# The last pair of a QKV projection: copy order, whole-block stores, and a remainder copied by two engines

## The chip, the cores and the metric

The kernel runs on one core of a Trainium2 chip. The metric is device time in microseconds of one execution. Engines: TensorE (PE in the profile; its weight loads are PEld), VectorE (DVE), ScalarE (ACT), GpSimd (POOL) and SyncE (SP), which computes nothing and issues most of the DMAs. ScalarE issues a few DMAs too; they stand in its own instruction order (ACTq in the profile, SPq for SP's).

## The reference

```python
batch, seq, hidden = 16, 512, 768
x     = np.random.randn(batch, seq, hidden).astype(np.float32)
w_qkv = np.random.randn(hidden, 3 * hidden).astype(np.float32)

qkv = np.matmul(x, w_qkv)
q, k, v = qkv[..., :768], qkv[..., 768:1536], qkv[..., 1536:]
return np.stack([q, k, v], axis=0)
```

An 8192 x 768 matrix times a 768 x 2304 matrix. The result is cut by columns into three outputs of 768 columns that lie one behind the other in memory.

## The kernel before

**Tiling.** The 8192 rows are taken in 32 pairs of 128-row tiles (`NP = 32`; a pair is 256 rows). The 2304 columns are taken as two wide groups of 1024 columns, columns 0 to 1023 and 1280 to 2303 (`Q_OFF = (0, 1280)`, two blocks of 512 each, `CB = 512`), and a remainder of 256 columns between them (`REM`). A pair and a wide group make a `quad`: a 2 x 2 block matrix with the blocks c11, c12, c21 and c22, each 128 rows x 512 columns, kept in one SBUF tile `u.o` until it is stored.

**Seven products.** A quad is computed by a Strassen-like scheme with seven half-depth products instead of eight. Products 1 and 2 use bf16 copies; products 3 to 7 use sums of weight blocks (`ts`) and sums of x blocks (`sr`). A product is three matmuls of 128x128 by 128x512 (`product`, L258). Products accumulate in PSUM banks: 1, 6, 7 and 4 in the bank `u.x`, 5 and 3 in `u.y`, 2 in `u.z`. `do(u, n)` runs one product and then copies or adds the bank to the block that it completes:

- product 1 is copied to c11 by ScalarE (L267), product 2 added to it by VectorE (L280);
- after product 6 the bank `u.x` is copied to c12 by ScalarE (L286); after product 3 VectorE adds `u.y` to c12 (L299);
- after product 7 ScalarE copies `u.x` to c22 (L292), and VectorE adds `u.y` (which holds product 5) to it (L293);
- after product 4 ScalarE copies `u.x` to c21 (L296).

**Order.** The instructions of each engine stand in the order in which the code issues them. Waits between engines are semaphores, put in from what each instruction reads and writes. Every DMA also takes one of eight completion semaphores in turn, and a DMA whose semaphore is still that of an earlier transfer waits, on the engine that issues it, until that one has landed.

**The end.** `plain` and `summed` handle the pairs in the middle. The two quads of the pair before the last are stored block by block with `store_cols` (from `plain` with `stored`, and from `summed` with `"parts"`). The last pair is `last(a, b)`: a is its columns 0 to 1023, b its columns 1280 to 2303. TensorE's order there is: product 1 of a and b, the remainder of the first row tile, product 2 of a and b, 6 of a and b, 5 and 7 of a, 5 and 7 of b, then 4 and 3 of a, 4 and 3 of b, and the remainder of the second row tile. Stores follow each finished block. `store_cols` cuts a block where it crosses from one of the three outputs into the next: c12 and c22 of a (columns 512 to 1023, a border at 768) and c11 and c21 of b (columns 1280 to 1791, a border at 1536) are two DMAs of 128x256 each. All go from SP, but c21 of a and the first half of c21 of b, which go from ScalarE. `rem_stored` computes the remainder of one row tile in six matmuls (L316), copies 128x256 with ScalarE (L414) and stores it from ScalarE (L416). L690 is the end of the program, where SP waits for all DMAs and the engines meet at a barrier.

Of the kernel before, what the change touches and what calls it, by code (L numbers as in the profile page):

```python
# [10 lines left out]
def kernel(  # L11
# [20 lines left out]
    nc = tc.nc  # L32
    P = 128
    G = 32
    B, T, H = x.shape
    M = B * T
# [5 lines left out]
    NP = M // (2 * P)  # L42
    CB = 512
    REM = N3 - 4 * CB
    Q_OFF = (0, 2 * CB + REM)
# [4 lines left out]
    ident = mybir.ActivationFunctionType.Identity  # L50
    add = mybir.AluOpType.add
# [3 lines left out]
    out_flat = out.rearrange("s b t h -> s (b t) h")  # L55
# [184 lines left out]
    def quad(p, q, pool=o_pool, tag="o"):  # L240
        u = Quad()
        u.p, u.q = p, q
        u.o = pool.tile([P, 2, 2 * CB], fp32, name="o", tag=tag)
        u.x = u.y = u.z = None
        return u

    def product(u, n, ps, start):
        t1, t2, t3, t4 = ts[u.q]
        if n <= 2:
            h = (n - 1) * KH  # L250
            lhs = [xb[u.p][:, h + j, :P] for j in range(KH)]
            rhs = [b1[u.q][:, h + j, :] for j in range(KH)]
        else:
            k, t = {3: (4, b22[u.q][:]), 4: (0, t4), 5: (1, t1), 6: (2, t2), 7: (3, t3)}[n]
            lhs = [sr[u.p][:, k, j, :] for j in range(KH)]
            rhs = [t[:, j, :] for j in range(KH)]
        for j in range(KH):
            nc.tensor.matmul(  # L258
                ps[:], lhs[j], rhs[j],
                start=(start and j == 0), stop=(j == KH - 1), skip_group_check=True,  # L260
            )

    def bank():
        return ps_pool.tile([P, CB], fp32, name="ps")

    def evacuate(u):
        nc.scalar.activation(u.o[:, 0, :CB], u.x[:], ident)  # L267

    def do(u, n, out=True):
        c11, c12 = u.o[:, 0, :CB], u.o[:, 0, CB:]  # L270
        c21, c22 = u.o[:, 1, :CB], u.o[:, 1, CB:]
        if n == 1:
            u.x = bank()
            product(u, 1, u.x, True)
            if out:
                evacuate(u)
        elif n == 2:
            u.z = bank()
            product(u, 2, u.z, True)
            nc.vector.tensor_tensor(c11, c11, u.z[:], op=add)  # L280
        elif n == 6:
            first = u.x is None
            if first:
                u.x = bank()
            product(u, 6, u.x, first)
            nc.scalar.activation(c12, u.x[:], ident)  # L286
        elif n == 5:
            u.y = bank()
            product(u, 5, u.y, True)
        elif n == 7:  # L290
            product(u, 7, u.x, False)
            nc.scalar.activation(c22, u.x[:], ident)  # L292
            nc.vector.tensor_tensor(c22, c22, u.y[:], op=add)  # L293
        elif n == 4:
            product(u, 4, u.x, False)
            nc.scalar.activation(c21, u.x[:], ident)  # L296
        elif n == 3:
            product(u, 3, u.y, False)
            nc.vector.tensor_tensor(c12, c12, u.y[:], op=add)  # L299
# [14 lines left out]
    def rem_row(p, r, ps):  # L314
        for j in range(KT):
            nc.tensor.matmul(  # L316
                ps, xb[p][:, j, r * P:(r + 1) * P], w_rem[j // KH][:, j % KH, :],
                start=(j == 0), stop=(j == KT - 1), skip_group_check=True,
            )
# [15 lines left out]
    def two(a, b, early, u=None):  # L335

        do(a, 1)
        do(b, 1, u is None)
        if u is None:
            early()  # L340
            rem(a.p)()()
        else:
            middle(u)
            copied = rem(a.p, between=lambda: third(u))
            evacuate(b)
            early()
            copied()()
            fourth(u)
            load_x(a.p + 3, nc.sync)
        do(a, 2)  # L350
        do(b, 2)
        summed(a, b)

    def summed(a, b, between={}, store=True):

        parts = {7: (1, CB, 2 * CB), 4: (1, 0, CB), 3: (0, CB, 2 * CB)}
        for i, (u, n) in enumerate(
            ((a, 6), (b, 6), (a, 5), (a, 7), (b, 5), (b, 7), (a, 4), (a, 3), (b, 4), (b, 3))
        ):
            do(u, n)  # L360
            if store == "parts" and n in parts:
                store_cols(u, *parts[n], nc.sync)
            elif n == 3 and store:
                store_quad(u)
            between.get(i, lambda: None)()
# [14 lines left out]
    def plain(a, b, c, d, early, rem_c, stored=False):  # L380

        add_first(a)
        add_first(b)
        rem(a.p)()()
        do(c, 1)
        do(d, 1)
        early()
        rem_c()
        do(c, 2)
        do(d, 2)  # L390
        add_second(a)
        add_second(b)
        if stored:
            for u in (c, d):
                store_cols(u, 0, 0, CB, nc.sync)

    def store_cols(u, r, lo, hi, *engs):

        c = Q_OFF[u.q] + lo
        end = Q_OFF[u.q] + hi  # L400
        while c < end:
            n = min(end, (c // H + 1) * H)
            row = (2 * u.p + r) * P
            engs[0].dma_start(
                out_flat[c // H, row:row + P, c % H:c % H + n - c],
                u.o[:, r, c - Q_OFF[u.q]:n - Q_OFF[u.q]],
            )
            c, engs = n, engs[1:] + engs[:1]

    def rem_stored(p, r):  # L410
        ps = bank()
        rem_row(p, r, ps[:, :REM])
        o = or_pool.tile([P, 2, REM], fp32, name="orem")
        nc.scalar.activation(o[:, 0, :], ps[:, :REM], ident)  # L414
        row = (2 * p + r) * P
        nc.scalar.dma_start(out_flat[1, row:row + P, R_OFF - H:R_OFF - H + REM], o[:, 0, :])  # L416

    def last(a, b):

        do(a, 1)  # L420
        do(b, 1)
        rem_stored(a.p, 0)
        for u in (a, b):
            do(u, 2)
            store_cols(u, 0, 0, CB, nc.sync)
        do(a, 6)
        do(b, 6)
        for u in (a, b):
            do(u, 5)
            do(u, 7)  # L430
            store_cols(u, 1, CB, 2 * CB, nc.sync)
        for u in (a, b):
            do(u, 4)
            store_cols(u, 1, 0, CB, *((nc.scalar, ) if u is a else (nc.scalar, nc.sync)))
            do(u, 3)
            store_cols(u, 0, CB, 2 * CB, nc.sync)
        rem_stored(a.p, 1)
# [132 lines left out]
    u = quad(2, 0)  # L570
# [72 lines left out]
    for p in range(ND + 3, NP - 1, 2):  # L643
        first = p == ND + 3
# [13 lines left out]
        a, b = quad(p, 0), quad(p, 1)  # L658
        summed(a, b, {5: turned} if first else {}, False)
        c, d = quad(p + 1, 0), quad(p + 1, 1)  # L660
        final = p + 3 >= NP
        plain(a, b, c, d, early, lambda: rem(c.p)()(), final)
        summed(c, d, {} if final else {0: lambda: transpose(p + 3, 2, 0)}, "parts" if final else True)
    last(quad(NP - 1, 0), quad(NP - 1, 1))


# [28 lines left out]
```

## Time and profile before

| what | value |
|---|---|
| time, median of 3 runs | 359.57 us (359.56 to 359.70) |
| the profiled execution's own time | 359.33 us |
| its span (first to last instruction on the core) | 357.5 us |
| TensorE busy | 352.0 us (98%) |
| VectorE busy | 263.9 us (74%) |
| ScalarE busy | 185.0 us (52%) |
| GpSimd busy | 177.3 us (50%) |
| DMA | 108.10 MB, mean 302 GB/s |
| granted TensorE clock | 1.0 |
| last product's matmuls and last remainder's end (ScalarE starts on it) | 353.73 us |
| stores of single blocks (L404) | 22 from SP, 2 from ScalarE |

How to read it: the times inside the profile count from the start of the span. 1.8 us of the profiled execution's time lie outside the span. A DMA-issuing instruction (DMA_DIRECT2D) shows how long the issuing engine was held, not how long the data took; the time from issue to landing is given by other views. In the views by stretch, the DMA share is the mean busy share of the 16 DMA engines and can come out a little over 1.

### The profile page before, as it was taken

To read this page: it belongs to the slowest core of one execution; us is meant where nothing else is said; L and a number is where in the kernel's file an instruction comes from. 1 tells how busy PE (TensorE), PEld (TensorE's weight loads), DVE (VectorE), ACT (ScalarE), POOL (GpSimd) and SP (SyncE) were. 2 spreads that over 40 slices of the span, in tenths; PEclk is the share of its full clock that TensorE was granted. 3 is DMA by queue.
4 is the path that set the end of the run, shared out by engine and by line. 5 is a ranking of instruction groups with operands and counts; after the bars stand their busy time and mean duration, and the time that the engine had idled before them with its cause. 6 is when DMAs were issued, how large, how long until landed. Compare 5 with 4: busy or idle time off the path is not lost.

```text
span 357.5 us, 5339 instructions
## 1 busy us (share of the span) xinstructions
PE 352.0 (98%) x1776; PEld 252.1 (71%) x1776; DVE 263.9 (74%) x308; ACT 185.0 (52%) x317; POOL 177.3 (50%) x184
## 2 busy tenths in 40 slices
PE   8999999999999999999999999999999999999995
PEld 3474677768677686877768677686877768677674
DVE  3789876796877869777695877869777695877643
ACT  4587755445454653645445454653645455454653
POOL 0031773376466453666535466453666535466420
PEclk9999999999999999999999999999999999999999
DMA  7997999999989998999979899798999979896497
GB/s 296 376 357 236 334 373 340 368 325 342 313 297 340 278 346 206 338 271 307 348 198 386 220 335 312 223 389 215 351 247 329 322 208 386 221 319 247 175 355 265
DMA packets 82203, 108.10 MB, mean 302 GB/s; under 512 B 5120, under 2 KB 62208, under 8 KB 82176
## 3 DMA queue, kind: packets, MB, share of 16 engines
q1 hardware_dynamic: 75072, 102.39, 85.6%
q10 hardware_dynamic: 7104, 5.38, 5.6%
q8 instruction: 14, 0.23, 0.3%
q14 instruction: 13, 0.11, 0.1%
HBM read 32.24 MB, written 75.50 MB: 301 GB/s over the span
## 4 chain that ended last, share of the span: by engine, by line
PE 97%; DMA 2%; ACT 0%; SPq 0%; issue 0%
PE ps L258 79%; PE ps L316 12%; PE ps L486 6%; DMA xin<-in_x_dram 2%; PE ps L185 0%; ACT xc L166 0%; SPq L162 0%; ACT orem L414 0%
## 5 line engine op out<-in xcount | busy, mean ns | idle before, releaser
L258 PE MATMUL ps<-t,s 128*128 128x512 f32 x720 | 177.9, 395 | 0.0
L258 PEld LDWEIGHTS ps<-t,s 128*128 128x128 f32 x720 | 135.0, 188 | 29.6 <-ACT o L267 0.2
L155 DVE STREAM_TRANSPOSE xf<-xin 128x768 f32<-128x768 f32 (+1 forms) x45 | 93.3, 2075 | 2.9 <-DMA xin<-in_x_dram 2.9
L258 PE MATMUL ps<-b,xb 128*128 128x512 bf16 x360 | 85.4, 380 | 0.0
L293 DVE TENSOR_TENSOR o<-o,ps 128x512 f32<-128x512 f32 x58 | 39.9, 687 | 55.2 <-ACT o L292 55.2
L205 POOL CAST xb<-xf 128x1536 bf16<-128x1536 f32 x28 | 41.1, 1466 | 57.0 <-DVE xf L155 57.0
L225 POOL TENSOR_TENSOR s<-xf 128x384 fp32r<-128x384 f32 x29 | 31.0, 1067 | 72.7 <-DVE xf L155 71.0
L258 PEld LDWEIGHTS <-xb 128*128 128x128 bf16 x360 | 33.9, 98 | 36.8 <-issue 4.2
L292 ACT ACTIVATE o<-ps 128x512 f32<-128x512 f32 x58 | 34.7, 598 | 43.6 <-PE ps L258 43.6
L299 DVE TENSOR_TENSOR o<-o,ps 128x512 f32<-128x512 f32 x60 | 41.1, 687 | 20.0 <-PE ps L258 18.8
L258 PE MATMUL ps<-b,s 128*128 128x512 f32 x180 | 50.6, 389 | 0.0
L296 ACT ACTIVATE o<-ps 128x512 f32<-128x512 f32 x60 | 35.9, 598 | 24.6 <-PE ps L258 22.1
L373 DVE TENSOR_TENSOR o<-o,ps 128x512 f32<-128x512 f32 x78 | 47.8, 681 | 0.0
L316 PE MATMUL ps<-w_rem,xb 128*128 128x256 bf16 x384 | 47.3, 273 | 0.0
L286 ACT ACTIVATE o<-ps 128x512 f32<-128x512 f32 x60 | 35.9, 599 | 19.2 <-PE ps L258 15.5
L316 PEld LDWEIGHTS <-xb 128*128 128x128 bf16 x384 | 37.4, 98 | 11.4 <-issue 0.5
L330 ACT ACTIVATE orem<-ps 128x512 f32<-128x512 f32 x31 | 18.5, 597 | 49.5 <-PE ps L316 35.2
L258 PEld LDWEIGHTS ps<-b,s 128*128 128x128 f32 x180 | 33.8, 188 | 7.1
L226 POOL TENSOR_TENSOR s<-s,xf 128x384 fp32r<-128x384 f32 x29 | 29.5, 1019 | 2.3
L227 POOL TENSOR_TENSOR s<-xf 128x384 fp32r<-128x384 f32 x29 | 29.5, 1016 | 0.0
L229 POOL TENSOR_TENSOR s<-xf,s 128x384 fp32r<-128x384 f32 x29 | 29.3, 1009 | 0.0
L377 ACT ACTIVATE o<-ps 128x512 f32<-128x512 f32 x26 | 15.5, 598 | 16.8 <-PE ps L258 16.1
(46 smaller groups left out, 158.6 us busy)
## 6 DMA issues: line engine op xcount, KB each, us to landing
out_dram<-o SPq DMA_DIRECT2D x60, 768.0 KB, 4.6
out_dram<-o SPq DMA_DIRECT2D x67, 256.0 KB, 3.7
xin<-in_x_dram SPq DMA_DIRECT2D x88, 192.0 KB, 5.7
out_dram<-orem SPq DMA_DIRECT2D x31, 256.0 KB, 2.3
xin<-in_x_dram ACTq DMA_DIRECT2D x24, 192.0 KB, 4.5
st<-in_w_qkv_dram SPq DMA_DIRECT2D x5, 768.0 KB, 8.0
out_dram<-o SPq DMA_DIRECT2D x15, 128.0 KB, 2.7
xin<-in_x_dram SPq DMA_DIRECT2D x2, 768.0 KB, 4.9
```

The source lines that it names most:

```text
L155: nc.vector.transpose(turned[:, g:g + n], rows[:, g:g + n])
L205: nc.gpsimd.tensor_copy(out=xb[p][:], in_=xf[p][:])
L225: 1: lambda g: g.tensor_tensor(s[:, 1], a21, a22, op=add),
L226: 2: lambda g: g.tensor_tensor(s[:, 2], s[:, 1], a11, op=sub),
L258: nc.tensor.matmul(ps[:], lhs[j], rhs[j], start=(start and j == 0), stop=(j == KH - 1), skip_group_check=True,)
L286: nc.scalar.activation(c12, u.x[:], ident)
L292: nc.scalar.activation(c22, u.x[:], ident)
L293: nc.vector.tensor_tensor(c22, c22, u.y[:], op=add)
L296: nc.scalar.activation(c21, u.x[:], ident)
L299: nc.vector.tensor_tensor(c12, c12, u.y[:], op=add)
L316: nc.tensor.matmul(ps, xb[p][:, j, r * P:(r + 1) * P], w_rem[j // KH][:, j % KH, :], start=(j == 0), stop=(j == KT - 1), skip_group_check= ...
L373: dve.tensor_tensor(c, c, u.z[:], op=add)
```

## The change

It has three parts, all in the last stretch of the program.

First, for the last pair only, c22 is put together in the other order. Product 5 is complete before product 7, so ScalarE copies `u.y` to c22 after product 5, and VectorE adds `u.x` after product 7.

Second, `store_cols` takes one engine and stores every block in one DMA. A block that crosses the border of two outputs is described as 128 rows x 2 pieces x 256 columns, where the step between the pieces leads from the end of a row in one output to the start of the same row in the next. It is also used for the pair before the last. In `last`, c21 of a is stored from ScalarE as before, and c21 of b whole from SP.

Third, `rem_stored`, which is used for the two row tiles of the last pair, copies the remainder's left 128 columns with ScalarE and its right 128 columns with VectorE; both read one PSUM bank. The store stays on ScalarE.

```diff
         elif n == 5:
             u.y = bank()
             product(u, 5, u.y, True)
+            if u.p == NP - 1:
+                nc.scalar.activation(c22, u.y[:], ident)
         elif n == 7:
             product(u, 7, u.x, False)
-            nc.scalar.activation(c22, u.x[:], ident)
-            nc.vector.tensor_tensor(c22, c22, u.y[:], op=add)
+            if u.p == NP - 1:
+                nc.vector.tensor_tensor(c22, c22, u.x[:], op=add)
+            else:
+                nc.scalar.activation(c22, u.x[:], ident)
+                nc.vector.tensor_tensor(c22, c22, u.y[:], op=add)
...
-    def store_cols(u, r, lo, hi, *engs):
+    def store_cols(u, r, lo, hi, eng):
 
         c = Q_OFF[u.q] + lo
-        end = Q_OFF[u.q] + hi
-        while c < end:
-            n = min(end, (c // H + 1) * H)
-            row = (2 * u.p + r) * P
-            engs[0].dma_start(
-                out_flat[c // H, row:row + P, c % H:c % H + n - c],
-                u.o[:, r, c - Q_OFF[u.q]:n - Q_OFF[u.q]],
-            )
-            c, engs = n, engs[1:] + engs[:1]
+        n = hi - lo
+        row = (2 * u.p + r) * P
+        src = u.o[:, r, lo:hi]
+        left = (c // H + 1) * H - c
+        if left >= n:
+            dst = out_flat[c // H, row:row + P, c % H:c % H + n]
+        else:
+            assert 2 * left == n
+            first = out_flat[c // H, row:row + P, c % H:H]
+            dst = bass.AP(first.tensor, first.offset, [[H, P], [M * H - H + left, 2], [1, left]])
+            src = src.rearrange("m (s n) -> m s n", s=2)
+        eng.dma_start(dst, src)
 
     def rem_stored(p, r):
         ps = bank()
         rem_row(p, r, ps[:, :REM])
         o = or_pool.tile([P, 2, REM], fp32, name="orem")
-        nc.scalar.activation(o[:, 0, :], ps[:, :REM], ident)
+        half = REM // 2
+        nc.scalar.activation(o[:, 0, :half], ps[:, :half], ident)
+        nc.vector.tensor_copy(out=o[:, 0, half:], in_=ps[:, half:REM])
...
-            store_cols(u, 1, 0, CB, *((nc.scalar, ) if u is a else (nc.scalar, nc.sync)))
+            store_cols(u, 1, 0, CB, nc.scalar if u is a else nc.sync)
```

## The prediction

> **What bounds the kernel now.** I read the chain of waits first, then the last 20 us in the timeline, then the same stretch cut into half microseconds, then the waits and landings of the stores. The chain, from the page:
>
> ```profile
> PE 97%; DMA 2%; ACT 0%; SPq 0%; issue 0%
> ```
>
> TensorE sets the time until its last matmul. The edits leave its instructions and their order alone, so only what follows it, and what prepares that, can move. The tail in the timeline:
>
> ```profile
> 348.98 0.60 ACT L292 ACTIVATE o<-ps 128x512 f32<-128x512 f32 x1 [0.76 <-PE ps L258]
> 349.61 0.69 DVE L293 TENSOR_TENSOR o<-o,ps 128x512 f32<-128x512 f32 x1 [2.62 <-ACT o L292]
> 350.34 0.60 ACT L292 ACTIVATE o<-ps 128x512 f32<-128x512 f32 x1 [0.76 <-PE ps L258]
> ...
> 350.97 0.69 DVE L293 TENSOR_TENSOR o<-o,ps 128x512 f32<-128x512 f32 x1 [0.67 <-ACT o L292]
> ...
> 353.06 0.69 DVE L299 TENSOR_TENSOR o<-o,ps 128x512 f32<-128x512 f32 x1 [0.67 <-PE ps L258]
> ...
> 353.73 0.38 ACT L414 ACTIVATE orem<-ps 128x256 f32<-128x256 f32 x1 [0.75 <-PE ps L316]
> 354.15 0.34 ACTq L416 DMA_DIRECT2D out_dram<-orem  x1
> ```
>
> See: each c22 is ready 0.60 + 0.03 + 0.69 us after its last product; c12 of b at 353.75; the remainder's store goes at 354.15. The half microseconds (from, to, length, busy times, clock, DMA share, GB/s):
>
> ```profile
> 350.50:351.00 0.50, 0.50 (x4) 0.42 (x3) 0.03 (x1) 0.44 (x1) 0.00 (x0) 1.00 0.06 23
> 351.00:351.50 0.50, 0.50 (x3) 0.39 (x3) 0.50 (x1) 0.48 (x1) 0.00 (x0) 1.00 0.64 229
> 351.50:352.00 0.50, 0.50 (x4) 0.41 (x3) 0.46 (x2) 0.12 (x1) 0.00 (x0) 1.00 0.76 264
> 352.00:352.50 0.50, 0.50 (x4) 0.42 (x3) 0.39 (x1) 0.12 (x1) 0.00 (x0) 1.00 0.11 33
> 352.50:353.00 0.50, 0.50 (x5) 0.23 (x4) 0.00 (x0) 0.48 (x1) 0.00 (x0) 1.00 0.94 369
> ...
> 356.00:356.50 0.50, 0.00 (x0) 0.00 (x0) 0.00 (x0) 0.00 (x0) 0.00 (x0) 1.00 0.44 164
> ```
>
> See: the DMA engines are nearly idle at 350.5 and at 352.0, then full from 352.5 without a gap until about 356.2 (the last row's 164 GB/s are 82 KB, 0.21 us at the 385 GB/s of the rows before it). So the end is a backlog of stores that began at 352.5: 1.4 MB, not one late instruction. From SP's waits and the landing view of the store issued at 354.52:
>
> ```profile
> SPq L404 <- DMA out_dram<-o: 0.7, 1, 0.7
> DMA to landing us min/median/max: 2.2/2.2/2.2
> ```
>
> The last store (c12 of b) was ready at 353.75, stood 0.7 us behind a reused completion semaphore, and landed at 356.7; the other 0.8 us to the span's end (357.5) is the closing barrier. What a merged store costs, by its nearest rows: the same shape (128x2x256, 256 KB), alone at 331.59:
>
> ```profile
> L331 SPq DMA_DIRECT2D out_dram<-orem x1: 373/373/373, 331.6 to 331.6; - x1
> DMA to landing us min/median/max: 2.1/2.1/2.1
> ```
>
> what the engines moved then (half-microsecond view, other bounds):
>
> ```profile
> 332.40:333.30 0.90, 0.90 (x11) 0.81 (x9) 0.90 (x2) 0.51 (x1) 0.00 (x0) 1.00 0.82 291
> ```
>
> and the four in a row on SP:
>
> ```profile
> 336.14 0.37 SPq L306 DMA_DIRECT2D out_dram<-o  x1
> 336.56 0.46 SPq L307 DMA_DIRECT2D out_dram<-o  x1
> 337.13 0.96 SPq L310 DMA_DIRECT2D out_dram<-o  x1
> 338.14 0.89 SPq L311 DMA_DIRECT2D out_dram<-o  x1
> ```
>
> See: alone it takes 0.37 us to issue, moves its bytes from 0.85 to 1.7 us after issue (0.9 us at 291 GB/s, not 385), and lands at 2.1; the third and fourth in a row hold SP for 0.9 each.
>
> **The change, part by part.** a and b are the two column halves of the last pair; times are of the profiled execution (span 357.5, 359.33 with what lies around it; the runs' median, 359.57, is 0.24 higher, and I carry differences over to it).
>
> *c22.* ScalarE copies the bank of product 5 while product 7 runs: 348.30 to 348.90 for a (products are 0.68 apart), and ScalarE is idle then. VectorE adds product 7's bank at 348.98 instead of 349.61, so c22 of a is ready at 349.67 (was 350.30), of b at 351.03 (was 351.66): 0.63 earlier each. The cover is 0.05 us thin (348.93 against 348.98), but if it is gone c22 is late by just that. New order to mind: product 4 now overwrites a bank that VectorE, not ScalarE, has read. Its earliest start is 350.34 for a, the read ends at 349.67; TensorE loses nothing. Nor does product 3, whose bank is read by 348.90.
>
> *One transfer for each block.* Four blocks of each pair straddle two outputs: the 24 stores of the last two pairs (22 from SP, 2 from ScalarE's queue) become 16, all but one from SP. The pair before the last is issued by 349 with or without this; its cost is nil while SP is free by 349.67 (now it is free from 349.3, and has less to do). In the last pair c22 of a is one issue (0.37) instead of two; c22 of b stays one and goes at 351.06 (was 351.69); c21 of a is unchanged on ScalarE's queue at 351.65; c12 of a goes at 352.42, as now, but whole; c21 of b, now halved between ScalarE's queue (353.01) and SP (353.36), goes whole from SP at 353.01. Behind it on SP waits c12 of b, ready at 353.75. With fewer stores the completion semaphore that it reuses belongs to a store that landed some 4 us before, so the 0.7 us wait goes; what is late next is SP's own issue or the backlog. c21's issue ends at 353.47 if it takes 0.46 as second in a row, at 354.0 if 0.96 as third: c12 of b goes at 353.78 or 354.0.
>
> *The remainder.* Two engines copy halves, but not side by side: as built, VectorE's half waits on the count that ScalarE's half raises, and the store waits on VectorE. ScalarE 128x128: 0.38 for 256 columns, 0.60 for 512, so 0.28. VectorE 128x128 from PSUM is in no row: 0.17 (a quarter of the 0.69 of 128x512) to 0.35 (a 128x384 copy from PSUM); I take 0.25, between casts of 384 and 512 columns drawn down to 128 (0.22) and the upper end. 353.73 + 0.28 + 0.03 + 0.25 + 0.03 = 354.32: the store goes 0.17 later than now (0.09 to 0.27). ScalarE has nothing behind it. The first remainder does the same at 345.0 with VectorE idle until 345.66: nil. The Trainium skill (PSUM — Partial Sum Buffer, PSUM bank collisions raise a hardware error) says that two engines may not read the same partitions of one bank at once, which speaks against the gain from two copiers; in parallel the copy would be 0.1 shorter than now. No run shows such a collision.
>
> *The sum.* Backlog by arrival, first bytes 0.85 after issue: c22 of a 350.5 to 351.4; c22 of b 351.9 to 352.5; c21 of a to 353.2; c12 of a can start at 353.3. So the 512 KB that now open the backlog at 352.5 are nearly out of the way, and about 0.5 us is won up to here. Then two merged stores follow each other from SP. If each moves its bytes in 0.87 to 0.9 as the lone one did, they end at 355.0 to 355.1; c12 of b and the remainder (393 KB at 385 GB/s: 1.02) drain by 356.03 to 356.12 against 356.21 now. Gain 0.09 to 0.18; I take 0.15: 359.57 - 0.15 = 359.42.
>
> **The rivals.** *The merged stores flow at full rate (−0.5).* For: the DMA engines, when full, carried 385 GB/s of 1 KB pieces too. Against: the lone store's 291. Then c12 of a drains at 353.98, c21 of b 354.66, c12 of b 355.34, the remainder 355.68: 0.53 less, 359.04. Its floor is the remainder: issued at 354.32, landing in 1.7 us at the soonest (what a 128 KB store at 350.33 took), 356.0 against 356.7, so at most 0.7 gained, 358.9. [...]
>
> *SP becomes the bound (slower).* c21 of b now stands wholly in front of c12 of b on SP. It decides from the point where the issues of c12 of a and c21 of b end after 354.52, when the last store goes now: 2.1 us for both. At the 0.9 of the third and fourth above they end by 354.4, just short. The same shape at L310 held SP for up to 1.86 us when the engines had a backlog: c21 of b would end at 354.9 to 355.3, c12 of b land 0.4 to 0.8 later than now: 360.0 to 360.4. Against: that is a third store in a row, c21 here a second.
>
> *The gap does not matter (no change).* If pieces of 1 KB set the pace everywhere, at 1.0 us per merged store, the drain ends at 356.3: 359.65.
>
> **How the numbers follow.** Paced merged stores, −0.2 to +0.1: 0.60 (the no-change rival is its upper edge). Full rate, −0.45 to −0.7: 0.25. SP-bound, +0.1 to +0.8: 0.15. Prediction 359.4; the range, 358.95 to 359.75, leaves out the bottom edge of the second and most of the third. About 0.2% (0.72 us) is what a measurement of this kernel can tell from no change: to gain that the remainder's floor must be beaten, 0.04; to lose that takes nearly the longest stall on record, 0.04; within it 0.92.
>
> **What would show it.** VectorE's add of c22 within 0.05 us of product 7's end, no ScalarE step between; SP issuing c22 of b near 351.06 and c12 of b near 353.8 with no semaphore wait; VectorE's half of the remainder starting after ScalarE's ends, store at 354.2 to 354.4; no DMA gap at 352.0, but a rate under 385 GB/s from 353.3 to 355. Full rate there means the first rival; a c21 issue over 1 us on SP the second. TensorE's last matmul off 353.7 by more than 0.1 would mean that something ahead of the tail moved, which I exclude.

## The result and the profile after

The changed kernel takes 358.94 us in the median, the kernel before 359.55 us beside it; the ratio is 0.9984, 95% interval 0.9978 to 0.9990. (One of the 22 executions of the kernel before took 737.67 us; the ratio leaves it out.) That is 0.61 us less, 0.16% by the ratio: in the predicted direction, within the 0.2% that was called no clear change, but four times the 0.15 us that was forecast. Carried over to 359.57, as the prediction does it, the saving gives 358.96, at the very edge of the stated range (358.95 to 359.75). The profiled execution's span fell from 357.5 to 357.0 us.

The tail of the changed kernel in the timeline (start, length, engine, line, operation; in brackets the idle time before it and what ended it):

```profile
348.28 0.60 ACT L291 ACTIVATE o<-ps 128x512 f32<-128x512 f32 x1
349.04 0.69 DVE L295 TENSOR_TENSOR o<-o,ps 128x512 f32<-128x512 f32 x1 [2.12 <-PE ps L258]
...
350.39 0.69 DVE L295 TENSOR_TENSOR o<-o,ps 128x512 f32<-128x512 f32 x1 [0.67 <-PE ps L258]
...
353.05 0.69 DVE L304 TENSOR_TENSOR o<-o,ps 128x512 f32<-128x512 f32 x1 [0.67 <-PE ps L258]
353.71 0.28 ACT L423 ACTIVATE orem<-ps 128x128 f32<-128x128 f32 x1 [0.75 <-PE ps L321]
354.02 0.29 DVE L424 COPY orem<-ps 128x128 f32<-128x128 f32 x1 [0.29 <-ACT orem L423]
354.35 0.34 ACTq L426 DMA_DIRECT2D out_dram<-orem  x1
```

ScalarE starts on the last remainder at 353.71, before the change at 353.73: TensorE did not move. VectorE's add to c22 begins at 349.04 and 350.39 instead of 349.61 and 350.97, right after product 7. The remainder's two copies stand one behind the other, and its store goes at 354.35, 0.2 us later than before.

The DMA traffic of the changed kernel by half microseconds (the last two columns are the share of the 16 DMA engines and GB/s):

```profile
351.50:352.00 0.50, 0.50 (x4) 0.42 (x3) 0.32 (x1) 0.10 (x1) 0.00 (x0) 1.00 0.10 37
352.00:352.50 0.50, 0.50 (x4) 0.42 (x3) 0.37 (x1) 0.14 (x1) 0.00 (x0) 1.00 1.01 393
352.50:353.00 0.50, 0.50 (x5) 0.23 (x4) 0.00 (x0) 0.46 (x1) 0.00 (x0) 1.00 1.06 406
353.00:353.50 0.50, 0.50 (x7) 0.36 (x4) 0.46 (x1) 0.00 (x0) 0.00 (x0) 1.00 0.91 338
353.50:354.00 0.50, 0.18 (x2) 0.00 (x0) 0.23 (x1) 0.28 (x1) 0.00 (x0) 1.00 1.07 377
354.00:354.50 0.50, 0.00 (x0) 0.00 (x0) 0.29 (x1) 0.00 (x0) 0.00 (x0) 1.00 1.10 387
354.50:355.00 0.50, 0.00 (x0) 0.00 (x0) 0.00 (x0) 0.00 (x0) 0.00 (x0) 1.00 1.10 406
...
355.50:356.00 0.50, 0.00 (x0) 0.00 (x0) 0.00 (x0) 0.00 (x0) 0.00 (x0) 1.00 0.48 164
```

The engines are full from 352.0, half a microsecond earlier than before, and empty at about 355.7 (164 GB/s in the last row are 0.21 us at full rate), also half a microsecond earlier. Between 353.3 and 355.0 the two merged stores of c12 of a and c21 of b and the start of c12 of b pass, from 353.5 on at 377 to 406 GB/s. The prediction had set 291 to 300 for them.

SP's waits in the same stretch hold no wait for a DMA in front of a store any more (L416 is the store; L700 is the end of the program):

```profile
SPq L700 <- DMA out_dram<-o: 1.6, 3, 0.6
SPq L416 <- DVE o L304: 1.2, 2, 0.9
```

### The profile page after: what moved, and what is told of

The parts are those of the page before. It is cut to its first block, busy times and chain, and to the rows that moved or that the text cites. A ratio compares the mean times of both kernels' runs of the same rounds, so it can differ in the third digit from the quotient of the medians.

```text
span 357.0 us, 5315 instructions
## 1 busy us (share of the span) xinstructions
PE 350.6 (98%) x1757; PEld 252.1 (71%) x1776; DVE 264.4 (74%) x310; ACT 185.0 (52%) x317; POOL 177.3 (50%) x184
## 4 chain that ended last, share of the span: by engine, by line
PE 74%; POOL 15%; DVE 6%; issue 3%; DMA 2%; ACT 0%; SPq 0%
PE ps L258 56%; PE ps L321 12%; PE ps L496 6%; DVE xf L155 6%; POOL xb L205 5%; POOL s L226 3%; POOL s L225 3%; POOL s L227 3%; DMA xin<-in_x_dram 2%; PE ps L185 0%; DVE o L304 0%; ACT xc L166 0%; SPq L162 0%; DVE orem L424 0%; ACT orem L423 0%
## 5 line engine op out<-in xcount | busy, mean ns | idle before, releaser
L258 PE MATMUL ps<-b,xb 128*128 128x512 bf16 x343 | 81.6, 379 | 1.1
L298 DVE TENSOR_TENSOR o<-o,ps 128x512 f32<-128x512 f32 x56 | 38.5, 688 | 50.7 <-ACT o L297 50.0
L304 DVE TENSOR_TENSOR o<-o,ps 128x512 f32<-128x512 f32 x60 | 41.1, 687 | 20.5 <-PE ps L258 19.4
L378 DVE TENSOR_TENSOR o<-o,ps 128x512 f32<-128x512 f32 x78 | 47.8, 680 | 0.0
```

Source lines behind the costliest of these rows:

```text
L258: nc.tensor.matmul(ps[:], lhs[j], rhs[j], start=(start and j == 0), stop=(j == KH - 1), skip_group_check=True,)
L378: dve.tensor_tensor(c, c, u.z[:], op=add)
```

## The experiments

Several kernels have their last matmul a few tenths of a microsecond earlier or later in the profiled execution, whatever their tail. So beside the time I compare the **tail**: from ScalarE's start on the last remainder to the end of the span. Each tail is that of one execution; three kernels whose times do not differ (before, whole-block stores alone, two copiers alone) agree within 0.04 us. All edits lie in the last pair's code or in the stores of the last two pairs. "Time" is the median against that of the kernel before in the same series.

| kernel | tail, us | time, us | ratio, 95% interval |
|---|---|---|---|
| before | 357.51 − 353.73 = 3.78 | | |
| changed | 357.02 − 353.71 = 3.31 | 358.94 (359.55) | 0.9984 (0.9978 to 0.9990) |
| c22 order alone | 357.47 − 354.02 = 3.45 | 359.12 (359.45) | 0.9993 (0.9984 to 1.0002) |
| whole-block stores alone | 357.63 − 353.81 = 3.82 | 359.45 (359.45) | 1.0001 (0.9992 to 1.0010) |
| two copiers alone | 357.96 − 354.14 = 3.82 | 359.52 (359.45) | 0.9999 (0.9991 to 1.0008) |
| changed, one copier | 357.52 − 354.21 = 3.31 | 358.92 (359.45) | 0.9985 (0.9976 to 0.9994) |
| changed, c22 of b stored late | 358.08 − 354.08 = 4.00 | 359.81 (359.69) | 1.0004 (0.9995 to 1.0013) |
| changed, blocks cut, all on SP | 358.12 − 354.29 = 3.83 | 359.73 (359.69) | 1.0003 (0.9994 to 1.0012) |
| changed, blocks cut, two queues | 357.94 − 354.49 = 3.45 | 359.48 (359.76) | 0.9992 (0.9983 to 1.0001) |
| products a, then b | 358.69 − 355.47 = 3.22 | 360.20 (359.69) | 1.0012 (1.0004 to 1.0021) |
| products by kind | 357.56 − 354.18 = 3.38 | 359.45 (359.75) | 0.9994 (0.9985 to 1.0003) |

The first theory, F: the end is a backlog of store traffic, and what counts is when its first bytes move. Its rivals: S, the gain comes from the completion semaphore on which the last store no longer waits; M, it comes from having one transfer per block.

### The c22 order alone

```diff
+            if u.p == NP - 1:                  # after product 5
+                nc.scalar.activation(c22, u.y[:], ident)
...
+            if u.p == NP - 1:                  # after product 7
+                nc.vector.tensor_tensor(c22, c22, u.x[:], op=add)
```

(added to the kernel before; the stores and the remainder as they were)

> Only the copy order of c22 is changed; blocks are cut into two stores as before, the remainder is copied by ScalarE alone. Theory F (the end is a backlog of bytes, and what counts is when its first bytes move): c22 of b is stored at about 351.1, the DMA engines are full from 351.9 and drained by about 355.7; 0.5 to 0.6 us under the kernel before, the whole gain of the full change. Theory S (the gain comes from the 0.7 us that c12 of b no longer waits for a reused completion semaphore): here the last store still reuses the semaphore of c21 of a, so less than 0.3 us. Theory M (one transfer per block is what pays): 0 to 0.2 us.

The tail is 3.45, 0.33 us of the whole 0.47, and the time 0.33 us less, with an interval that just touches 1. The traffic of this kernel (here ScalarE starts on the remainder at 354.02):

```profile
352.00:352.50 0.50, 0.50 (x4) 0.40 (x3) 0.50 (x1) 0.00 (x0) 0.00 (x0) 1.00 0.48 188
352.50:353.00 0.50, 0.50 (x4) 0.35 (x2) 0.18 (x1) 0.33 (x1) 0.00 (x0) 1.00 1.06 410
...
353.50:354.00 0.50, 0.48 (x5) 0.19 (x2) 0.50 (x1) 0.00 (x0) 0.00 (x0) 1.00 0.87 305
354.00:354.50 0.50, 0.00 (x0) 0.00 (x0) 0.04 (x1) 0.38 (x1) 0.00 (x0) 1.00 0.90 316
```

The backlog starts half a microsecond earlier, as F says, but has a hole around 354.0, where the first half of c12 of a has passed and its second half is not there yet. So F gets most of it, and something is left that the merged stores add.

### Whole-block stores alone

```diff
-    def store_cols(u, r, lo, hi, *engs):      # as in the change: one DMA per block,
+    def store_cols(u, r, lo, hi, eng):        # c21 of b from SP
```

> Only the whole-block stores; c22 in the old order, the remainder copied by ScalarE alone. The last store reuses a semaphore that has long landed, so its 0.7 us wait is gone. Theory F: the backlog still begins at 352.5 with the same bytes and drains at 356.2; within 0.1 us of the kernel before. Theory S: 0.5 us faster. Theory M: 0.4 to 0.6 us faster.

Nothing is gained. SP's waits and the traffic of this kernel:

```profile
SPq L411 <- DVE o L293: 0.9, 1, 0.9
SPq L411 <- DVE o L299: 0.6, 2, 0.3
```

```profile
352.00:352.50 0.50, 0.50 (x4) 0.38 (x4) 0.47 (x1) 0.04 (x1) 0.00 (x0) 1.00 0.09 27
352.50:353.00 0.50, 0.50 (x4) 0.24 (x3) 0.00 (x0) 0.50 (x1) 0.00 (x0) 1.00 0.73 287
...
356.00:356.50 0.50, 0.00 (x0) 0.00 (x0) 0.00 (x0) 0.00 (x0) 0.00 (x0) 1.00 0.73 252
```

The 0.7 us wait for a reused semaphore is gone (no store waits for a DMA), the last store goes earlier, and the end does not move, since the bytes in front of it still start after 352.5. Neither S nor M gives a gain on its own.

### Two copiers alone, and the change without them

```diff
-        nc.scalar.activation(o[:, 0, :], ps[:, :REM], ident)
+        nc.scalar.activation(o[:, 0, :half], ps[:, :half], ident)
+        nc.vector.tensor_copy(out=o[:, 0, half:], in_=ps[:, half:REM])
```

> Only the remainder copied by two engines. The copies stand one behind the other: 0.28 us on ScalarE, then 0.29 on VectorE, store about 0.2 us later than before. Theory F: hidden behind the backlog, 0 within 0.1 us. If the last store's issue sets the end rather than the backlog: 0.2 us slower.

> The changed kernel, with the remainder copied by ScalarE alone again. Its store goes 0.2 us earlier (354.13 against 354.35). Theory F: the DMA engines are full until 355.7 either way, so the time is that of the changed kernel within 0.1 us. If the remainder's chain is the floor, as in the first rival, 0.2 us faster than the changed kernel.

Added alone: tail 3.82 against 3.78, time 0.07 us up, in the noise. Taken out of the change: tail 3.31 in both. The third part of the change makes the remainder's store 0.2 us later and costs nothing that shows here, as F said: the engines are still busy with blocks when it comes.

### c22 of b ready early, stored late

```diff
         for u in (a, b):
             do(u, 5)
             do(u, 7)
-            store_cols(u, 1, CB, 2 * CB, nc.sync)
+            if u is a:
+                store_cols(u, 1, CB, 2 * CB, nc.sync)
...
             store_cols(u, 0, CB, 2 * CB, nc.sync)
+            if u is a:
+                store_cols(b, 1, CB, 2 * CB, nc.sync)
```

> The changed kernel, but the store of c22 of b is issued behind the store of c12 of a, though its data is ready as early as in the changed kernel. Nothing else moves on VectorE or ScalarE. Tail below: from ScalarE's start on the last remainder to the end of the span, 3.78 us before the change, 3.31 with it. Theory F (when the backlog's first bytes move): the 0.5 us hole in the DMA traffic is back, the tail is 3.75 to 3.9 and the time that of the kernel before within 0.15 us. If the shorter chain of copies pays by itself: 3.3, the time of the changed kernel.

The gain is gone: tail 4.00, time 0.12 us above the kernel before, within the noise. The traffic (remainder at 354.08):

```profile
352.00:352.50 0.50, 0.50 (x4) 0.42 (x3) 0.45 (x1) 0.00 (x0) 0.00 (x0) 1.00 0.01 4
352.50:353.00 0.50, 0.50 (x4) 0.38 (x2) 0.24 (x1) 0.27 (x1) 0.00 (x0) 1.00 0.21 86
353.00:353.50 0.50, 0.50 (x5) 0.26 (x4) 0.09 (x1) 0.33 (x1) 0.00 (x0) 1.00 1.06 406
353.50:354.00 0.50, 0.50 (x6) 0.24 (x3) 0.50 (x1) 0.00 (x0) 0.00 (x0) 1.00 0.71 246
```

The hole before the backlog is back, and a second one appears at 353.5: 246 GB/s in place of 385 for half a microsecond is 0.18 us, which would account for the 0.1 by which the tail is above what F had at most. SP also has one store more in its last row, and c12 of b goes 0.20 us after ScalarE's start on the remainder instead of 0.05, so not all of the loss need be the hole. The shorter chain of copies gains nothing by itself. What pays is the store that it lets go earlier.

### Blocks cut again, on one queue and on two

```diff
-        eng.dma_start(dst, src)               # one DMA per block
+        while c < end:                        # store_cols of the kernel before:
+            n = min(end, (c // H + 1) * H)    # two DMAs for a straddling block
...
             # first kernel: c21 of b, both halves
             store_cols(u, 1, 0, CB, nc.scalar if u is a else nc.sync)
             # second kernel: its first half from ScalarE
             store_cols(u, 1, 0, CB, *((nc.scalar, ) if u is a else (nc.scalar, nc.sync)))
```

(in the changed kernel, c22 order and two copiers kept)

> The changed kernel with each straddling block in two DMAs of 128x256 again, both from SP; five stores then stand on SP in the last microseconds. Theory F: the bytes and their start are the same, so the tail is 3.3 to 3.45 (small holes of 0.1 us between a first half and the rest are possible, as in the kernel with the c22 order alone). Theory M2 (with c22 early, SP's issues become the bound and merging is needed): c12 of b goes 0.4 us later than in the changed kernel, tail 3.6 or more.

F in its simple form fails here: same bytes, same start, and the tail is 3.83. M2 comes out: c12 of b goes 0.60 us after ScalarE's start on the remainder (354.89 against 354.29), in the changed kernel 0.05 after it, so 0.55 later where 0.4 was expected. The traffic when all halves come from SP:

```profile
352.50:353.00 0.50, 0.50 (x4) 0.41 (x3) 0.44 (x1) 0.06 (x1) 0.00 (x0) 1.00 0.96 377
353.00:353.50 0.50, 0.50 (x4) 0.24 (x3) 0.00 (x0) 0.50 (x1) 0.00 (x0) 1.00 1.09 418
...
354.00:354.50 0.50, 0.25 (x3) 0.00 (x0) 0.30 (x1) 0.21 (x1) 0.00 (x0) 1.00 0.78 273
354.50:355.00 0.50, 0.00 (x0) 0.00 (x0) 0.29 (x1) 0.06 (x1) 0.00 (x0) 1.00 0.76 264
355.00:355.50 0.50, 0.00 (x0) 0.00 (x0) 0.00 (x0) 0.00 (x0) 0.00 (x0) 1.00 0.73 254
355.50:356.00 0.50, 0.00 (x0) 0.00 (x0) 0.00 (x0) 0.00 (x0) 0.00 (x0) 1.00 0.81 283
```

and the issues on SP, the two halves of c12 of a, the two of c21 of b, and c12 of b (start, how long SP is held):

```profile
352.97 0.33 SPq L409 DMA_DIRECT2D out_dram<-o  x1
353.35 0.44 SPq L409 DMA_DIRECT2D out_dram<-o  x1
353.89 0.40 SPq L409 DMA_DIRECT2D out_dram<-o  x1
354.34 0.46 SPq L409 DMA_DIRECT2D out_dram<-o  x1
354.89 0.41 SPq L409 DMA_DIRECT2D out_dram<-o  x1
```

The backlog starts early, and then the engines run at 254 to 283 GB/s for two microseconds. Through this stretch SP does nothing but issue: from the end of one issue to the start of the next there are 0.05 to 0.1 us, though the data are ready (ScalarE has copied c21 of b by 353.54, VectorE has completed c12 of b by 354.31). A half goes out every 0.38 to 0.55 us, and its 131 KB keep the engines busy for only 0.34 us at 385 GB/s. The four halves land at 354.70, 355.16, 355.66 and 356.17, each 1.7 to 1.8 us after its issue, as the store at 350.33 of the kernel before did (1.7). So none of them stands behind another: the engines wait for SP. A whole block holds SP for 0.37 us and brings 262 KB, 0.68 us of work for the engines; in the changed kernel two of them land at 354.53 and 355.20, 391 GB/s. To test this, one store was moved to the other queue. The expectation takes the half microsecond for a pace of the queue (theory D) instead of SP's issuing:

> The changed kernel with blocks cut into two stores again, and the first half of c21 of b back on ScalarE's queue: it differs from the kernel with all halves on SP in the issuing engine of one store. That kernel had a tail of 3.83 us (ScalarE's start on the last remainder to the span's end), the one with the c22 order alone 3.45, the changed one 3.31. Theory D (a queue takes one small store each 0.5 us, so four halves in a row on SP move 128 KB per 0.5 us and leave the DMA engines a third idle): with one of them on the other queue the tail is 3.4 to 3.5. If the cut itself costs (more and smaller stores, whoever issues them): 3.8.

Tail 3.45, time 0.28 us under the kernel before (the interval reaches 1.0001): the cut costs 0.52 us on one queue, 0.14 on two. D forecast this, and SP's issuing forecasts the same: SP has one issue less, and c12 of b goes 0.10 us after ScalarE's start on the remainder. This run cannot tell the two apart; the landings above, which follow each issue without delay, speak for SP's issuing. The Trainium skill (DMA: Bandwidth & Descriptors, Issuing engines are not separate DMA queues) says that transfers from all engines run on the same 16 DMA engines, so that issuing from several saves only sequencer time. Here that time was what counted: with 131 KB stores SP alone left about a third of the engines' 385 GB/s unused.

### Other orders of the products

Two kernels try to have blocks ready earlier, so that fewer bytes are left at the end; both copy the remainder with ScalarE alone.

```diff
-        do(a, 6)
-        do(b, 6)
-        for u in (a, b):
-            do(u, 5)
-            do(u, 7)
...
+        for u in (a, b):        # first kernel: 5, 6, 3, 7 of a, then of b; 4 of a, 4 of b
+            do(u, 5)
+            do(u, 6)
+            do(u, 3)
+            do(u, 7)
...
+        for n in (6, 5):        # second kernel: 6, 5, 7, 3, 4, each of a, then of b
+            do(a, n)
+            do(b, n)
```

> The changed kernel with the products of the last pair in another order (2 of a and b, then 5, 6, 3, 7 of a, 5, 6, 3, 7 of b, 4 of a, 4 of b, remainder) and the remainder copied by ScalarE alone, so that c12 and c22 of a are stored while the DMA engines are idle otherwise. Theory F: 512 KB fewer are left in the backlog; it is drained by about 355.4 against 355.7, and the remainder's store becomes the last link: tail about 3.0 to 3.1, 0.25 us under the changed kernel. TensorE may stall 0.1 us in front of product 4 of b, since VectorE reads its bank until then. If the backlog is not what sets the end: no change.

Slower by 0.5 us. The tail is shorter, 3.22 (3.0 to 3.1 was expected), but ScalarE reaches the last remainder at 355.47: TensorE's weight loads waited for the engines that read a bank before the next product may overwrite it. (The second row names no releaser; it stands at 348.35 in front of product 3 of a, the same place at which b waits for ScalarE's L291.)

```profile
PEld ps L258 <- DVE o L295: 0.5, 1, 0.5
PEld ps L258 <- issue: 0.5, 1, 0.5
PEld ps L258 <- ACT o L291: 0.4, 1, 0.4
...
PEld ps L258 <- ACT o L286: 0.2, 1, 0.2
```

I had expected a stall of 0.1 us, and only in front of product 4 of b. One product (0.68) stands between, against a copy of 0.60 or an add of 0.69; the hand-overs on both sides do not fit into what is left.

> The changed kernel with the last pair's products taken kind by kind (2, 6, 5 of a and b as pairs, then 7 of a and b, 3 of a and b, 4 of a and b, remainder), so that two other products stand between one that fills a bank and the next one that overwrites it, and one block becomes ready every 0.7 us; the remainder is copied by ScalarE alone. Expected if a steady stream of blocks is what the end needs: no stall of TensorE, the DMA engines full from about 2.6 us before ScalarE starts on the last remainder, drained 1.8 us after it (2.0 with the change), tail 3.05 to 3.15 us against 3.31, 0.2 us under the changed kernel. If the last remainder's own store is already what ends the program, 3.2 to 3.3.

Here TensorE waits for no copy. The engines are full from 351.6, 2.6 us before the remainder, as expected, but the tail is 3.38, and 0.3 us are gained over the kernel before (the interval reaches 1.0003), less than with the change. ScalarE's order, and the traffic behind it:

```profile
352.64 0.60 ACT L301 ACTIVATE o<-ps 128x512 f32<-128x512 f32 x1 [2.80 <-PE ps L258]
...
353.26 0.37 ACTq L416 DMA_DIRECT2D out_dram<-o  x1
353.68 0.60 ACT L301 ACTIVATE o<-ps 128x512 f32<-128x512 f32 x1 [0.45 <-PE ps L258]
354.18 0.38 ACT L422 ACTIVATE orem<-ps 128x256 f32<-128x256 f32 x1
```

```profile
355.00:355.50 0.50, 0.00 (x0) 0.00 (x0) 0.00 (x0) 0.00 (x0) 0.00 (x0) 1.00 0.62 215
```

ScalarE issues the store of c21 of a between its two last block copies. The issue holds it for 0.37 us, the copy of c21 of b starts late by as much, and the remainder behind it by 0.2. The store of c21 of b is late with it, and the engines run short of work at 355.0. No version that I ran beats the changed kernel. Leaving the second copier out of it is as good.

## Why the prediction was right and wrong

**Right.** What bounds the end: a backlog of store traffic, fed from the moment at which c22 of b is stored. The late store of c22 of b shows it, and the whole-block stores alone show that the semaphore wait in front of the last store was not on the path. c22 is ready 0.57 to 0.58 us earlier instead of 0.63, because VectorE starts 0.06 later behind product 7 than ScalarE did. That is not the thin cover that the prediction named: ScalarE's copy ended at 348.88, 0.16 before VectorE began, and the wait that ended last was the one for TensorE. In front of each of the two adds VectorE has an instruction that only waits (an EVENT_SEMAPHORE on L295), which the adds of c22 in the kernel before do not have; whether the 0.06 is its cost was not tried. The remainder's copies are serial, VectorE's half takes 0.29 against 0.25 taken, and its store goes at 354.35 against 354.32. c12 of b goes at 353.76 (353.78 was forecast). TensorE did not move.

**Wrong in size.** The failed step is the sum's last one: "If each moves its bytes in 0.87 to 0.9 as the lone one did, they end at 355.0 to 355.1". Back to back the second merged store landed 0.67 us after the first. A store that is alone shows 0.9 us from its first to its last byte; that this is no rate was to be seen in the same row, where the DMA engines are 82% busy over the stretch. Without its first and last 0.2 us the same lone store runs at full rate:

```profile
332.60:333.10 0.50, 0.50 (x7) 0.44 (x5) 0.50 (x2) 0.31 (x1) 0.00 (x0) 1.00 1.09 389
```

The other row that the prediction leaned on, four two-piece stores of which the third and fourth held SP for 0.9 us each, says how long SP is held, and not that bytes arrive more slowly: in the changed kernel the last stores stand 0.6 to 0.8 us apart, each holds SP for 0.34 to 0.37 us, and the engines stay at 338 to 406 GB/s from 352.0 until the backlog runs out. With 0.68 in place of 0.87 to 0.9 the sum gives the first rival: drained at 355.68, 359.04 us; measured about 355.7 and 358.94. That rival had been given 0.25. That the range still reaches the saving, by 0.01 us, is luck: its lower edge was drawn inside the first rival's interval, and the reckoning that led to 359.4 does not reach it.

**Not seen.** The prediction gave the merging no gain of its own, only less for SP to issue. With c22 early it is needed: on top of the c22 order it takes the tail from 3.45 to 3.31, and it is what allows c21 of b to go to SP at all. With c21 of b cut and wholly on SP the gain is lost again (3.83), because then SP's issuing sets the pace. That was the second rival's mechanism; the prediction looked for it at whole blocks, where it did not show.

## What to carry to other kernels

At the end of a program look at the DMA traffic by half microseconds, find where the last uninterrupted stretch begins, and ask which store starts it. Here making that store 0.6 us earlier shortened the end by 0.33, and by 0.47 once the stores behind it kept the engines full, while a shorter wait or copy behind it was worth nothing. A lone transfer's time from first to last byte is not its rate in a stream. And one engine that issues many small stores may feed the DMA engines too slowly even when no issue looks long: compare the bytes of a store, divided by the time from one issue to the next, with the full rate.

## What the runs showed of the hardware

- A store of 131 KB in 128 pieces of 1 KB held SP for 0.33 to 0.46 us, and in a row SP issued one every 0.38 to 0.55 us, while its bytes need 0.34 us at 385 GB/s; the engines then ran at 254 to 283 GB/s. A store of 262 KB in 256 pieces of the same 1 KB held SP for 0.37 us, and the second of two landed 0.67 us after the first, 391 GB/s. Why some issues take 0.40 to 0.46 us and not 0.33 was not tried.
- A DMA issue on ScalarE holds its next copy for 0.37 us; in one kernel the copy of the last remainder came 0.2 us late by it, though ScalarE is half idle over the whole span.
- Between a product, the copy that empties its bank, and the next product into that bank, one other product (0.68 us) was not enough to hide a copy of 0.60 us: TensorE's weight loads waited 0.4 us for one and 0.2 us for another.
